# A Conformer layer's depthwise convolution: two channel tiles on TensorE by diagonal matrices become five by quads of taps, and three groups of w_mod go to VectorE

## The chip, the core and the metric

The kernel runs on one core of a Trainium2 chip. The metric is the time of one execution on the device, in microseconds (us). The core's engines are TensorE (PE, matrix products), VectorE (DVE), ScalarE (ACT), GpSimd (POOL) and SyncE (SP, which issues most DMAs). Each has its own queue of instructions and runs it in order; semaphores join them.

## The reference, cut to what matters

Two layers over 256 positions of 2048 channels in float32. Layer 0 mixes positions with a Conformer convolution module, layer 1 with a Mamba-2 mixer; behind each stands a squared-ReLU MLP of 8192 hidden channels. A vector c gives shift, scale and gate of each sub-layer. The change is in layer 0's mixer and in a part of the vectors from c:

```python
mod = (sc @ w_mod[i] + b_mod[i])[:, None, :]            # sc = silu(c)
sh1, sc1, g1, sh2, sc2, g2 = jnp.split(mod, 6, axis=-1)
u = rmsnorm(h, norm_mix_g[i]) * (1 + sc1) + sh1
v = u @ w_pw1 + b_pw1                                   # 2048 -> 4096
a, gt = jnp.split(v, 2, axis=-1)
v = a * jax.nn.sigmoid(gt)
v = causal_dwconv(v, w_dw, b_dw)                        # 31 taps, each channel by itself
v = jax.nn.silu(layernorm(v, ln_g, ln_b))
mix = v @ w_pw2 + b_pw2
h = h + g1 * mix
```

## The kernel before

Channels lie on the 128 partitions and the 256 positions along the free axis, so 2048 channels are sixteen tiles ct of 128x256. The first pointwise product runs in float32 (`native`, L649): eight blocks b of 512 output columns, which are the two halves (value and gate) of two channel tiles. A block has four steps g of four input tiles each, sixteen products, and a 1 MB load `w` from `pw`. Blocks 0 to 2 run while the first shifts and scales arrive; then block 3, and blocks 4 to 7 one after another. `glu` (L567, L569) closes a channel tile: ACT takes the sigmoid of the gate, DVE multiplies and writes to `vpad`, which has 30 zeros ahead of the 256 positions, so that tap k is the slice that begins at k.

`conv(ct)` is the convolution. Of 31 taps ACT makes 24 as scaled copies, four to a 128x1024 buffer (L580), DVE adds these buffers (L596, wide adds), adds the last seven taps one by one (L599), and folds four into one (L603, L605, the adder tree). The last two tiles, 14 and 15, come out of block 7: there PE takes 13 taps as products with diagonal matrices (`diag`, L592), ACT 12 and DVE 6. `close(ct, y)` subtracts a common estimate of the mean, which is tile 0's sum over channels by a product with ones (L614, L616), from each tile (L617), and ACT squares it (L621). `moments` (L631) sums tiles and squares over channels by products with ones, in four column slices of 32, one group of four tiles at a time; the last four tiles are added singly (L737), after the row sums (L726, L730). From these DVE and ACT make mean and deviation (L740 to L748), and `normed` scales, applies the SiLU and splits a group of four tiles into a high and a low part (L757 to L763, L464, L465). The second pointwise product (`pw2`, `outer`, then `block`, L355) multiplies those by split weights (L340, L342).

Beside it runs w_mod: a job is one load of 128x2048 and its product with silu(c). In most groups of four jobs DVE does it in one instruction a job (L271). In the groups listed in PE_GROUPS PE does it with four products of 32 columns and 512 positions (L262), and after the fourth a copy (L268), four transposes (L283) and a sum (L285) bring the row to columns. Jobs are taken from a list, EARLY first: gate g1's groups 0 to 2 and sc2's group 0 beside blocks 3 to 7 (RATE_PW1: 16 jobs in 20 steps), g1's group 3 and sh2's group 0 (BETWEEN: 8 jobs) between the statistics and pw2, and one job a step beside pw2. Before the change all groups of g1 and sh2 of layer 0 are PE's.

All loads of weights go through `stream` (L326) on SP's queue in the order of the program: a load that waits for its buffer, or for its source, holds up those behind it. Buffers are three for `w`, two for `wm`, four for `hid` (w_mod jobs use wm, hid, hid in turn). A scheduler orders each engine's instructions when the program is built, from the order of the code, priorities (`high_priority`) and `issue_after`.

## Time and profile before

| | |
|---|---|
| median of 3 runs | 2610.81 us (2610.38 to 2611.61) |
| the profiled execution | 2609.13 us |
| its span | 2607.2 us, 36320 instructions |
| PE busy | 2541.3 us, 97% |
| DVE, ACT, POOL busy | 1945.7, 1363.9, 132.5 us |
| DMA | 659.10 MB, 253 GB/s in the mean |
| mean granted clock of TensorE | 0.988 |
| PE products of `native` (L649) | 1024 rows, 232.3 us |
| ACT taps (L580) | 360, 148.2 us |

Times are us from the span's start. In a timeline row stand start and length, engine, line, operation, output and inputs, shapes and a count xN; a bracket holds the idle time ahead of it and what ended it. A float32 product shows as two rows of PE, so x32 is sixteen products. A length reaches to the modelled end of a product, and the next one starts before it, so what products cost is read from start to start. In a table of stretches stand length, busy time and count for PE, weight loads, DVE, ACT and POOL, then the granted clock (1.00 is full), the share of time in which the DMA engines were busy, and GB/s.

### The profile page before, as it was taken

What the parts mean: (1) busy time and instruction counts of PE and PEld (TensorE: products, weight loads), DVE (VectorE), ACT (ScalarE), POOL (GpSimd) and SP (SyncE); (2) the same over time, 40 slices, a digit from 0 to 9 for tenths busy, and PEclk for the clock granted to TensorE, in tenths of its full rate; (3) what the DMA queues carried; (4) which work ended last, traced back from release to release, by engine and by line L of the source; (5) the groups of instructions that cost most, each with busy time, mean ns of one, the idle gap of its engine ahead of it and who ended that gap; (6) DMA issues with size and microseconds to landing.
All of it is one profiled execution on the core that took longest, in us unless ns stands there. A gap on an engine that the chain in (4) does not pass through costs nothing.

```text
span 2607.2 us, 36320 instructions
## 1 busy us (share of the span) xinstructions
PE 2541.3 (97%) x14291; PEld 2180.5 (84%) x14291; DVE 1945.7 (75%) x2558; ACT 1363.9 (52%) x2145; POOL 132.5 (5%) x170
## 2 busy tenths in 40 slices
PE   6999999999999999999999999999999999999998
PEld 4877798888888888888888888888998888888886
DVE  6689977677888878887877777888885565565565
ACT  2099754444434434447777666744454344443443
POOL 0000000000000000000000000000000101101000
PEclk8999999999999999999999999999999999999999
DMA  9876797588888888866555455688775555555553
GB/s 406 345 278 252 279 376 285 218 337 320 314 323 328 314 307 334 312 225 220 182 188 184 166 182 182 234 305 317 285 263 189 192 193 190 185 191 194 187 186 144
DMA packets 92878, 659.10 MB, mean 253 GB/s; under 512 B 10497, under 2 KB 10497, under 8 KB 14753
## 3 DMA queue, kind: packets, MB, share of 16 engines
q1 hardware_dynamic: 89138, 644.53, 65.6%
q0 software_dynamic: 3136, 10.59, 1.4%
q8 instruction: 112, 1.84, 0.3%
q10 hardware_dynamic: 432, 1.66, 0.2%
q14 instruction: 60, 0.49, 0.1%
HBM read 654.53 MB, written 2.20 MB: 252 GB/s over the span
## 4 chain that ended last, share of the span: by engine, by line
PE 87%; DVE 6%; DMA 3%; ACT 2%; issue 1%; POOL 0%; ACTq 0%; DVEq 0%; SPq 0%; POOLq 0%
PE mm L355 57%; PE mm L409 8%; PE mm L411 8%; PE mm L410 8%; PE mm L649 3%; ACT taps L580 2%; DMA hid<-wmT 1%; DVE taps L596 1%; DVE wl L342 1%; DVE taps L599 1%; DMA wm<-wmT 1%; DVE hid L271 1%; DVE wm L271 1%; PE ms L262 1%; DMA t<-eac_d 0%
## 5 line engine op out<-in xcount | busy, mean ns | idle before, releaser
L355 PE MATMUL mm<-u,wh 128*128 128x512 f32 (+1 forms) x4544 | 1376.1, 365 | 6.9 <-ACT u L467 3.4
L342 DVE TENSOR_TENSOR wl<-w,wh 128x1024 fp32r<-128x1024 f32 x768 | 940.7, 1228 | 513.5 <-ACT wh L340 510.3
L340 ACT CAST wh<-w 128x1024 fp32r<-128x1024 f32 x768 | 806.8, 1051 | 980.6 <-PE mm L355 602.5
L355 PE MATMUL mm<-u,wl 128*128 128x256 f32 x3840 | 1078.9, 282 | 0.1
L355 PEld LDWEIGHTS mm<-u,wh 128*128 128x128 f32 x4544 | 812.8, 190 | 160.2 <-issue 12.8
L355 PEld LDWEIGHTS mm<-u,wl 128*128 128x128 f32 x3840 | 729.8, 190 | 6.6 <-issue 2.5
L409 PE MATMUL mm<-wh,hid 128*128 128x512 f32 x896 | 350.7, 391 | 0.0
L411 PE MATMUL mm<-wh,hid 128*128 128x512 f32 x896 | 348.8, 389 | 0.0
L410 PE MATMUL mm<-wl,hid 128*128 128x512 f32 x896 | 348.7, 389 | 0.0
L271 DVE SCALAR_TENSOR_TENSOR wm<-wm,scb 128x2048 f32<-128x2048 f32 x128 | 292.3, 2283 | 8.2 <-DMA wm<-wmT 8.2
L649 PE MATMUL mm<-u,w 128*128 128x256 f32 x1024 | 232.3, 388 | 26.7 <-ACT u L560 25.1
L649 PEld LDWEIGHTS mm<-u,w 128*128 128x128 f32 x1024 | 197.6, 195 | 64.9 <-ACT u L560 26.6
L409 PEld LDWEIGHTS mm<-wh,hid 128*128 128x128 f32 x896 | 168.2, 188 | 35.7 <-issue 1.0
L410 PEld LDWEIGHTS mm<-wl,hid 128*128 128x128 f32 x896 | 168.2, 188 | 35.4 <-issue 0.7
L411 PEld LDWEIGHTS mm<-wh,hid 128*128 128x128 f32 x896 | 168.2, 188 | 35.2
L355 PE MATMUL mm<-hid,wh 128*128 128x512 f32 (+1 forms) x576 | 182.5, 373 | 2.4 <-DVE acc L837 2.4
L580 ACT ACTIVATE taps<-u,par 128x256 f32<-128x256 f32 x360 | 148.2, 500 | 3.6 <-DVE taps L596 2.2
L355 PE MATMUL mm<-hid,wl 128*128 128x256 f32 x512 | 143.8, 281 | 0.0
L355 PEld LDWEIGHTS mm<-hid,wh 128*128 128x128 f32 x576 | 104.1, 188 | 23.1 <-DVE acc L837 2.7
L299 POOL TENSOR_TENSOR mod<-mod,par 128x4 f32<-128x4 f32 x46 | 39.8, 864 | 1319.3 <-DVE wm L271 885.1
L355 PEld LDWEIGHTS mm<-hid,wl 128*128 128x128 f32 x512 | 96.9, 189 | 0.4 <-issue 0.2
L596 DVE TENSOR_TENSOR taps<-taps,taps 128x1024 f32<-128x1024 f32 x74 | 90.1, 1218 | 8.7 <-ACT taps L580 7.8
(241 smaller groups left out, 1562.9 us busy)
## 6 DMA issues: line engine op xcount, KB each, us to landing
w<-w SPq DMA_DIRECT2D x256, 1024.0 KB, 4.9
wm<-wmT SPq DMA_DIRECT2D x140, 1024.0 KB, 7.0
w<-win SPq DMA_DIRECT2D x80, 1024.0 KB, 4.9
hid<-wmT SPq DMA_DIRECT2D x52, 1024.0 KB, 10.6
w<-pw SPq DMA_DIRECT2D x48, 1024.0 KB, 5.3
w<-wout SPq DMA_DIRECT2D x32, 1024.0 KB, 6.9
acc<-ac_d POOLq DMA_DIRECT2D x16, 512.0 KB, 7.7
h<-xT SPq DMA_DIRECT2D x4, 512.0 KB, 6.2
```

Source lines behind the costliest of these rows:

```text
L262: self.pe = nc.tensor.matmul(self.row_sums[32 * t:32 * t + 32, :], lhsT=self.scol[:, kt:kt + 1].broadcast_to([P, 32]), rhs=w[:, t * 512:(t ...
L271: self.sum = nc.vector.scalar_tensor_tensor(out=w, in0=w, scalar=1.0, in1=self.scb, op0=ALU.mult, op1=ALU.mult, accum_out=m[:, i:i + 1]).ins
L299: nc.gpsimd.tensor_tensor(out=m, in0=m, in1=b, op=ALU.add)
L340: nc.scalar.copy(out=wh, in_=w[:, s, :])
L342: nc.vector.tensor_tensor(out=wl, in0=w[:, s, :], in1=wh.bitcast(F32), op=ALU.subtract)
L355: self.pe = self.nc.tensor.matmul(out, lhsT=lhsT, rhs=rhs, skip_group_check=True, **kw).ins
L409: mm(banks[q], lhsT=hi, rhs=wh[:, k, :], start=g == 0 and t == 0, stop=False)
L410: mm(banks[q], lhsT=hi, rhs=wl[:, k, :], start=False, stop=False)
L411: mm(banks[q], lhsT=lo, rhs=wh[:, k, :], start=False, stop=g == 3 and t == 3)
L580: st["tap"] = nc.scalar.activation(out=p4[:, q, :], in_=vp[:, k + q:k + q + T], func=AF.Identity, scale=self.col("w_dw", ct * TAPS + k + q ...
L596: nc.vector.tensor_add(wide, wide, products(four("wl"), k))
L649: self.pe = nc.tensor.matmul(o, lhsT=w[:, t, j * P:(j + 1) * P], rhs=u[g][:, t, :], start=g == 0 and t == 0 and j < 2, stop=g == 3 and t == 3,
```

## The change

Five channel tiles, 4, 8, 12, 14 and 15, are convolved on PE alone, all 31 taps and a zero one. For such a tile the 128 rows of a product are 32 channels times four copies of their row, shifted by 0, 8, 16 and 24 taps: `shift` makes the copies with four DMAs from `vpad` to 32 partitions each. The weights (`quad`) hold four taps of each of 32 channels. A tile is eight taps k times four groups c of 32 channels, 32 products of 128 rows, 32 columns and 256 positions (`convolve`); the four groups go to four column slices. The channels of these tiles lie in another order, in which the parameters and the rows of pw2 are laid out on the host. `close` takes PE's result with the bias. The other eleven tiles have 28 taps on ACT and 3 on DVE. PE_GROUPS loses g1's groups 0 to 2, so those twelve jobs are DVE's. Of pw2's first loads one goes ahead of the last shifts, the other two behind four and eight jobs of BETWEEN. The copies use the memory of `xpad`, which layer 1 needs later.

```diff
-ACT_TAPS = 24
-DIAG, PE_TAPS, FEW_TAPS = 2, 13, 12
+ACT_TAPS = 28
+TE_ROWS = (4, 8, 12, 14, 15)
+LONG = T + 7
...
-PE_GROUPS = {(0, G1, g) for g in range(4)} | {(0, SH2, g) for g in range(4)}
+PE_GROUPS = {(0, G1, 3)} | {(0, SH2, g) for g in range(4)}
...
+        self.xpad = self.const("xpad", [P, 5 * (3 + T)])
...
-        W = T + TAPS - 1
+        W = T + TAPS
...
+            nc.gpsimd.memset(v[:, W - 1:], 0.0)
...
+        quad = self.b("acc", [P, 8, P], bufs=5)
+        copies = self.xpad[:, :4 * LONG].rearrange("p (c t) -> p c t", c=4)
+        parts = {}
...
-            with self.tc.high_priority(AHEAD_GLU):
+            with self.tc.high_priority(AHEAD_GLU if ct < NT - 2 else AHEAD_CHAIN):
...
-            few = ct >= NT - DIAG
-            k0, k1 = (PE_TAPS, PE_TAPS + FEW_TAPS) if few else (0, ACT_TAPS)
+            k0, k1 = 0, ACT_TAPS
...
+        def weigh(ct, w):
+            self.stream(w, a["quad"][TE_ROWS.index(ct)])
+        def shift(ct, r):
+            for i in range(4):
+                self.stream(r[32 * i:32 * i + 32], vpad[ct % 12][:, 8 * i:8 * i + LONG])
+        def convolve(ct, w, r):
+            o = parts[ct] = self.bank(self.mm, "mm")[:, :T]
+            with self.tc.issue_after(self.pe):
+                for k in range(8):
+                    for c in range(4):
+                        self.pe = nc.tensor.matmul(o[32 * c:32 * c + 32, :], lhsT=w[:, k, 32 * c:32 * c + 32],
+                                                   rhs=r[:, c, k:k + T], start=k == 0, stop=k == 7,
+                                                   skip_group_check=True).ins
...
-            self.sub = nc.vector.tensor_sub(d, y, st["m0"]).ins
+            if ct in parts:
+                self.sub = nc.vector.scalar_tensor_tensor(out=d, in0=parts[ct], scalar=self.col("b_dw", ct),
+                                                          in1=st["m0"], op0=ALU.add, op1=ALU.subtract).ins
+            else:
+                self.sub = nc.vector.tensor_sub(d, y, st["m0"]).ins
...
+                    if row and g == 2:
+                        weigh(row, quad)
+                        shift(row, copies)
                     load(0, g)
                     self.pump(pump(g))
+                    if row and g == 3:
+                        convolve(row, quad, copies)
+                        if row == 12:
+                            weigh(14, quad)
                     products(0, g, 0, 4)
...
-        native([FIRST], glu, pump=pump, hook=lambda: close(0, y))
...
+        native([FIRST], glu, pump=pump, hook=lambda: close(0, y), row=4)
+        for b, rows in ((4, (1, 2, 3, 4)), (5, (5, 6)), (6, (7, 8, 9)), (7, (10, 11, 13))):
+            for ct in rows:
+                close(ct, None if ct in parts else conv(ct))
             if b >= 6:
                 moments(b - 6)
...
+            native([b], glu, pump=pump, row={5: 8, 7: 12}.get(b))
...
+        there = [self.load_w(a["pw2"][0, 0])]
+        shift(14, copies)
+        quad15 = self.wp.tile([P, 8, P], F32, tag="wh", name=self.nm("taps"), bufs=3)
+        weigh(15, quad15)
+        copies15 = self.b("hid", [P, 4, LONG])
+        shift(15, copies15)
+        close(12, None)
+        convolve(14, quad, copies)
         moments(2)
...
+        rows = self.t("t2", [P, 2 * T], bufs=3)
+        nc.scalar.copy(out=rows, in_=st["sums"])
+        convolve(15, quad15, copies15)
+        close(14, None)
+        close(15, None)
...
-        there = [self.load_w(a["pw2"][b, 0]) for b in range(3)]
...
-            self.pump(BETWEEN)
+            for b in (1, 2):
+                self.pump(BETWEEN // 2)
+                there.append(self.load_w(a["pw2"][b, 0]))
```

How instructions move is seen best in the engines' orders as the program is built. First VectorE at the convolution of tile 0 (`taps_595` before, `taps_609` now; `taps_746` and `taps_790` are tile 1's), before and now:

```order
L596 TENSOR_TENSOR taps_595<-taps_595,taps_618 128x1024
L596 TENSOR_TENSOR taps_595<-taps_595,taps_624 128x1024
L599 SCALAR_TENSOR_TENSOR taps_595<-u_161,par,taps_595 128x256 x7
L596 TENSOR_TENSOR taps_746<-taps_746,taps_751 128x1024
L603 TENSOR_TENSOR taps_595<-taps_595 128x512
L596 TENSOR_TENSOR taps_746<-taps_746,taps_757 128x1024
L605 TENSOR_TENSOR taps_595<-taps_595 128x256
```

```order
L604 TENSOR_TENSOR taps_609<-taps_609,taps_632 128x1024
L282 SCALAR_TENSOR_TENSOR wm_677,mod_679<-wm_677,scb 128x2048
L604 TENSOR_TENSOR taps_609<-taps_609,taps_638 128x1024
L604 TENSOR_TENSOR taps_609<-taps_609,taps_644 128x1024
L607 SCALAR_TENSOR_TENSOR taps_609<-u_162,par,taps_609 128x256 x3
L604 TENSOR_TENSOR taps_790<-taps_790,taps_795 128x1024
L609 TENSOR_TENSOR taps_609<-taps_609 128x512
L604 TENSOR_TENSOR taps_790<-taps_790,taps_801 128x1024
L611 TENSOR_TENSOR taps_609<-taps_609 128x256
```

The first w_mod job (L282, on `wm_677`) now stands ahead of tile 0's last wide adds, of which there is one more, and three single taps remain of seven. Next TensorE from the last step of block 7 to the start of the last statistics (`xpad` are the copies of tile 14, `hid_1758` those of tile 15):

```order
L649 MATMUL mm_1648<-u_164,w_251_1719 128x256 x8
L631 MATMUL ms_1379<-acc_179,ones 32x256 x4
L631 MATMUL ms_1379<-sq_1330,ones 32x256
L631 MATMUL ms_1379<-sq_1377,ones 32x256
L631 MATMUL ms_1379<-sq_1539,ones 32x256
L631 MATMUL ms_1379<-sq_1586,ones 32x256
L592 MATMUL ms_1806<-u_161,hid_1643 128x256 x13
L592 MATMUL mm_1851<-u_162,hid_1645 128x256 x13
L730 MATMUL mm_1894<-t_268_1849,bT_116 128x512
```

```order
L677 MATMUL mm_1614<-u_165,w_245_1684 128x256 x8
L628 MATMUL mm_1766<-xpad,acc_194 32x256 x32
L659 MATMUL ms_1359<-acc_192,ones 32x256 x4
L659 MATMUL ms_1359<-sq_1308,ones 32x256
L659 MATMUL ms_1359<-sq_1357,ones 32x256
L659 MATMUL ms_1359<-sq_1505,ones 32x256
L659 MATMUL ms_1359<-sq_1554,ones 32x256
L628 MATMUL mm_1809<-hid_1758,taps_1756 32x256 x32
L764 MATMUL mm_1848<-t_256_1807,bT_117 128x512
```

The moments of the third group, first before, stand between the two convolutions now, and the row sums (L764, L730 before) behind the second as they did. Last TensorE from the last statistics to pw2's first products (`mm_1997`, `mm_1949`; `ms_` are w_mod's):

```order
L737 MATMUL mm_1894<-nrm_1892,ones 128x256
L262 MATMUL ms_1944<-hid_1941,scol 32x512 x4
L262 MATMUL ms_1944<-wm_1949,scol 32x512 x4
L262 MATMUL ms_1944<-hid_1955,scol 32x512 x4
L262 MATMUL ms_1944<-wm_1961,scol 32x512 x4
L262 MATMUL ms_1972<-hid_1969,scol 32x512 x4
L262 MATMUL ms_1972<-wm_1977,scol 32x512 x4
L355 MATMUL mm_1997<-u_1920,wh_1937 128x256
```

```order
L770 MATMUL mm_1848<-nrm_1846,ones 128x256
L273 MATMUL ms_1892<-hid_1889,scol 32x512 x4
L273 MATMUL ms_1892<-hid_1897,scol 32x512 x4
L273 MATMUL ms_1892<-wm_1903,scol 32x512 x4
L273 MATMUL ms_1892<-hid_1909,scol 32x512 x4
L366 MATMUL mm_1949<-u_1868,wh_1885 128x256
```

Six w_mod jobs stood ahead of pw2's first product, four do now; the other two join the two that stand among the products.

More of the change, by code (lines that the diff above doesn't have):

```diff
@@ L102, in layout @@
     head[:HEADS, 1] = a["mb_a_log"].reshape(-1)
+    order = np.arange(D).reshape(NT, P)
+    for ct in TE_ROWS:
+        order[ct] = order[ct].reshape(32, 4).T.reshape(-1)
+    order = order.reshape(-1)
     par = np.concatenate([
@@ L136, in layout @@
         "wmT": wmt,
[L137 removed]
+        "pw1": _tiles(pw1), "pw2": _tiles(a["cf_w_pw2"][0][order]),
         "wdt": np.ascontiguousarray(wdt.reshape(NT, P, P).transpose(1, 0, 2)),
@@ L987, in mamba @@
         self.time_steps(u)
-        self.xpad = [self.one.tile([P, 3 + T], F32, tag=f"xpad{i}", name=f"xpad{i}") for i in range(5)]
+        self.xpad = [self.xpad[:, i * (3 + T):(i + 1) * (3 + T)] for i in range(5)]
         for v in self.xpad:
```

47 lines of the change are left out of this document (11 added, 36 removed).

## Prediction

> **What bounds the kernel now.** The busy time by stretch comes first, cut where the Conformer's work changes: pointwise blocks 3 to 7 with the convolution, the convolution's tail, the second pointwise product. The columns are TensorE (PE), weight loads, VectorE (DVE), ScalarE (ACT), GpSimd, granted clock, DMA share, GB/s.
>
> ```profile
> 136.00:292.00 156.00, 156.00 (x782) 124.68 (x782) 150.01 (x228) 149.24 (x371) 8.03 (x9) 1.00 0.67 258
> 292.00:311.00 19.00, 17.16 (x88) 13.42 (x86) 16.09 (x29) 13.09 (x30) 0.00 (x0) 1.00 0.82 332
> ...
> 320.00:425.00 105.00, 104.99 (x858) 95.28 (x858) 75.35 (x97) 52.62 (x80) 7.83 (x10) 1.00 0.91 360
> ```
>
> From 136 to 292 three engines are full at once: PE 156.0 us of 156, DVE 150.0, ACT 149.2. Relief for DVE and ACT alone moves nothing there. From 320 to 425 PE is full again, so what the stage wins must survive PE's work behind it. Then the PE timeline of the tail:
>
> ```profile
> 292.23 0.64 PE L631 MATMUL ms<-acc,ones 128*32 128x256 f32 x8
> ...
> 293.23 5.88 PE L592 MATMUL ms<-u,hid 128*128 128x256 f32 x26
> 298.95 5.78 PE L592 MATMUL mm<-u,hid 128*128 128x256 f32 x26
> 304.56 1.02 PE L730 MATMUL mm<-t,bT 128*128 128x512 f32 x2
> 305.42 0.59 PE L737 MATMUL mm<-acc,ones 128*128 128x256 f32 x2
> 305.85 0.59 PE L737 MATMUL mm<-lo,ones 128*128 128x256 f32 x2
> ...
> 310.55 0.61 PE L737 MATMUL mm<-nrm,ones 128*128 128x256 f32 x2
> ...
> 313.69 1.04 PE L262 MATMUL ms<-wm,scol 128*32 128x512 f32 x8
> 314.55 1.04 PE L262 MATMUL ms<-hid,scol 128*32 128x512 f32 x8
> ...
> 320.01 0.39 PE L355 MATMUL mm<-u,wh 128*128 128x256 f32 x1 [0.62 <-DVE u L465]
> ```
>
> Blocks end at 292.23, the two diagonal convolutions at 304.56; the last of eight pairs of statistics (L737) starts at 310.55, and 9.5 us later (320.01) the first normalised tile lets PE run on.
>
> **TensorE until block 7 ends.** The prices are in the timeline's early rows.
>
> ```profile
> 135.90 7.14 PE L649 MATMUL mm<-u,w 128*128 128x256 f32 x32 [1.66 <-DMA w<-pw]
> 142.97 1.06 PE L262 MATMUL mm<-wm,scol 128*32 128x512 f32 x8
> 143.97 7.17 PE L649 MATMUL mm<-u,w 128*128 128x256 f32 x32
> 150.98 0.59 PE L614 MATMUL ms<-taps,ones 128*128 128x256 f32 x2
> ...
> 191.81 0.66 PE L283 MATMUL mm<-ident,t 128*128 128x128 f32 x4
> 192.30 7.07 PE L649 MATMUL mm<-u,w 128*128 128x256 f32 x32
> ```
>
> A step of sixteen products takes 7.0 us (143.97 to 150.98), a w_mod job 1.0 (142.97 to 143.97), the transpose of a job's rows 0.5. Removed before 292: twelve jobs and three transposes, 13.5 us. Added: three convolutions (tiles 4, 8, 12).
>
> A convolution is eight groups of four products with 32 columns each. No row shows one, but w_mod's job is such a group with 512 columns: they follow one another every 0.86 us (313.69 to 314.55), so 0.43 for 256; and the moments (L631), two groups of 256 columns, take 1.00 with the change of kind in it (292.23 to 293.23). A job alone between full products takes 1.00, so going to column slices and back costs 0.14. I take 8 x 0.43 + 0.14 = 3.6 us. Bounds: 3.4 without the 0.14, and 32 x 0.43 = 13.8 if nothing overlapped, from which the 0.86 rows are far. The Trainium skill (TensorEngine Tiling, Key Properties) says that a change of tiling mode drains TensorE, and gives no time. The 0.14 is what these rows leave for it.
>
> New in this stretch is one wait. The first product of statistics (L614) stands behind block 3's second step and needs tile 0's sum. Without the w_mod job PE is there at 135.90 + 14.0 = 149.9. The other engines have more to do first. ACT's timeline, DVE's, DVE's groups in this stage, and the page's group for w_mod:
>
> ```profile
> 134.65 16.56 ACT L580 ACTIVATE taps<-u,par 128x256 f32<-128x256 f32 x41
> ```
> ```profile
> 148.34 0.68 DVE L603 TENSOR_TENSOR taps<-taps 128x512 f32<-128x512 f32 x1
> 148.94 1.22 DVE L596 TENSOR_TENSOR taps<-taps,taps 128x1024 f32<-128x1024 f32 x1
> 150.07 0.42 DVE L605 TENSOR_TENSOR taps<-taps 128x256 f32<-128x256 f32 x1
> ```
> ```profile
> L596 DVE TENSOR_TENSOR taps<-taps,taps 128x1024 f32<-128x1024 f32 x74 | 90.1, 1218 | 8.7 <-ACT taps L580 7.8
> L599 DVE SCALAR_TENSOR_TENSOR taps<-u,par,taps 128x256 f32<-128x256 f32 x110 | 45.1, 477 | 0.4
> ```
> ```profile
> L271 DVE SCALAR_TENSOR_TENSOR wm<-wm,scb 128x2048 f32<-128x2048 f32 x128 | 292.3, 2283 | 8.2 <-DMA wm<-wmT 8.2
> ```
>
> A tap costs ACT 16.56 / 41 = 0.404, a wide add DVE 1.13 (148.94 to 150.07), a half add 0.6, a single tap 45.1 / 110 = 0.41, a w_mod job 2.28. ACT had three taps done by 134.65, so its twentieth is at 141.5. From there DVE's new order is add, w_mod job, two adds, three taps, add, half add, add, quarter add: 1.13 + 2.28 + 2.26 + 1.23 + 1.13 + 0.6 + 1.13 + 0.42 = 10.2, so 151.7. PE waits 1.8 us (0 to 2.5, by how the adds follow ACT).
>
> Block 7's end, E: 135.90 + 20 x 7.0 + 1.8 + 0.6 (L614) + 2.0 (two moments) + 3 x 3.6 = 291.1, where it was 292.23.
>
> **ScalarE and VectorE.** ACT loses 52 of 360 taps, 21 us. DVE goes from 74 to 66 wide adds (-9.0), from 110 to 33 single taps (-31.6) and loses five adder trees (about -5) for twelve w_mod jobs (+27.4). Its list until tile 12 is closed: eleven convolutions at 6 x 1.13 + 3 x 0.41 + 1.3 = 9.3, sixteen jobs at 2.28, 4 us of gates and closes: 143 us from 136.8. With 2 us of early waits and 4 for tile 13, whose taps start only after block 6, it ends near 286. Tile 14's gate is due at E - 2.8 = 288.3: 2 us of cover.
>
> **The loads.** A shift is four DMAs on SP's queue, and each convolution has one of weights: 25 issues in place of 2. The queue's own rows, its longest wait in 100 to 330, and the small landings:
>
> ```profile
> 292.75 0.38 SPq L326 DMA_DIRECT2D hid<-wmT  x1
> ```
> ```profile
> SPq L326 <- PE mm L649: 179.2, 26, 15.2
> ```
> ```profile
> ac_d<-wm POOLq DMA_DIRECT2D x1, 64.0 KB, 3.6
> eac_d<-wm POOLq DMA_DIRECT2D x1, 32.0 KB, 1.8
> ```
>
> At 0.38 us an issue that is 9 us on a queue that waited 179 for PE to free buffers, and 3.6 MB more where DMA was a third idle (0.67). Until block 7 ends it is hidden: the pointwise loads queued behind a shift go out some 20 us (three steps) ahead of use. In the tail it is not. I take 2.5 us from the last issue to landing, between 1.8 and 3.6. Tile 14: gate done at E - 2.3, four issues, landed at E + 1.5. Tile 15: gate done at E + 1.3, landed at E + 5.
>
> **The tail.** PE idles to E + 1.5, convolves tile 14 to E + 5.1, makes the last moments to E + 6.1, convolves tile 15 (landed by then) to E + 9.7; then in order L730 (0.86) and seven pairs (0.43 each). The last pair starts at E + 13.6 = 304.7, where it was 310.55: 5.9 us earlier. The closes of tiles 14 and 15 are hidden by those pairs; what is late next is PE's own list.
>
> **What is given back.** The first normalised tile follows at 304.7 + 9.5 = 314.2. Before it PE did six w_mod jobs, now four, so two (2.0 us) fall into the stretch where PE is full. And the four end at 304.7 + 0.6 + 3.5 = 308.8, so PE stands nearly still for 5.4 us. What that does to the clock shows elsewhere, in the timeline, the stretch and the chain around 430:
>
> ```profile
> 428.58 0.67 PE L482 MATMUL ms<-diag,ones 128*128 128x256 f32 x2 [1.10 <-DVE diag L478]
> ```
> ```profile
> 430.00:440.00 10.00, 9.29 (x54) 8.99 (x55) 8.25 (x12) 3.17 (x6) 0.00 (x0) 0.67 0.54 211
> ```
> ```profile
> 431.94 13.32 PE mm L355 x92
> 445.69 11.51 PE mm L355 x96
> ```
>
> After some 4 us with little more than that 0.67 the clock was 0.67 over the next 10 us, and 92 products took 13.3 us where 96 took 11.5: 2.3 us lost. Between 315.6 and 320, with a w_mod job halfway, it held. The new gap is longer and emptier: I take 2.3, bounds 0 and 3.3.
>
> **Sum:** -5.9 + 2.0 + 2.3 = -1.6 us. The profiled execution took 2609.13 us (span 2607.2); the median of the runs, 2610.81, is 1.7 above. Forecast 2609.2. A measurement of this kernel tells about 0.2%, 5.2 us, from no change, so this is no change. It is passed on whole: PE is full until 425, and the loads keep up (the fourteenth megabyte issued after 294, the first that PE meets in the product's second step, is in by 329 at 2.5 us each, used near 336).
>
> **Rivals.**
> *The tail wins whole.* If the clock holds and tile 0's sum is in time, 2.3 and 1.8 are not lost: -5.7, 2605.1, faster. For it: the gap at 315 kept the clock. Against: the new one has less work in it. 0.18.
> *Column groups overlap by three quarters:* 0.57 a group, five convolutions 5.7 us longer, 2614.9, still no change. The 0.86 rows are against it; that no row has more than five such groups in a line leaves room. 0.10. The Trainium skill (TensorE: Matmul & The Clock Gate, Measured speedup vs the span model) has three column tiles at 2.38 times one, 79%, which would add 4.5 us.
> *Only two of four overlap:* 0.86 a group, 7.0 us a convolution, five times 3.4: +17, 2626, slower. It decides from 5.0 us a convolution on. For it: weights change with every one of the 32 products, four times as many as in the moments. 0.10.
> *VectorE becomes the bound:* a w_mod job stands ahead of adds and gates; if its load is late, ACT's buffers fill and PE waits for gates. Past the 2 us of cover each is one of time, and from 9 late it is slower: 2609 to 2620. For it, 150.0 of 156; against, the shorter list. 0.12, half of it slower.
> *The change doesn't do what it says:* its new order has the jobs off PE and five convolutions on it, which rules this out.
> The forecast has 0.50. Faster 0.18; same 0.50 + 0.10 + 0.06 = 0.66; slower 0.10 + 0.06 = 0.16. Its own range is -5 to +3. To hold 8 in 10 the range takes in a tail with both gains and 1.5 us of earlier landing (2603.5) and most of a late VectorE (2617), and leaves out the 2626.
>
> **What would show it.** Convolutions of 3.6 us, 7 by the third rival; PE idle 1.8 us before its first statistics; block 7 done near 291; the last pair near 304.7; a clock below 1 after 310, held by the first rival; VectorE idle before tile 14's gate, busy up to it by the fourth. I am wrong if PE waits for a load in blocks 3 to 7, or if a shift lands later than 4 us.

## The result, and the profile after

The changed kernel took 2626.49 us (median of six runs, 2623.09 to 2631.66); the kernel before took 2610.60 beside it (2609.96 to 2611.76). The ratio is 1.0062 (95% interval 1.0049 to 1.0076): 16 us slower, where 2609.2 was forecast and no change. The profiled execution took 2630.72 us (span 2628.9), 21.6 more than the one of before, and it is that difference which the traces can explain.

The same three stretches of the kernel after, in the columns of before:

```profile
136.00:292.00 156.00, 144.68 (x760) 121.62 (x761) 139.83 (x168) 134.95 (x337) 5.17 (x6) 0.96 0.70 256
292.00:311.00 19.00, 15.53 (x132) 11.14 (x134) 7.31 (x10) 4.20 (x7) 0.59 (x3) 0.91 0.59 159
320.00:425.00 105.00, 96.58 (x738) 82.71 (x738) 73.07 (x94) 49.21 (x81) 4.91 (x10) 0.95 0.88 343
```

TensorE was full in the first and the third; now it lacks 11.3 and 8.4 us there, and VectorE and ScalarE are less busy than before. So no engine took TensorE's place as the bound: it waits. Where, its timeline tells:

```profile
136.78 14.05 PE L677 MATMUL mm<-u,w 128*128 128x256 f32 x64 [1.88 <-DMA w<-pw]
153.65 1.11 PE L638 MATMUL ms<-taps,ones 128*128 128x256 f32 x2 [2.82 <-DVE taps L611]
154.55 8.39 PE L677 MATMUL mm<-u,w 128*128 128x256 f32 x32
162.88 3.67 PE L628 MATMUL mm<-xpad,acc 128*32 128x256 f32 x64
166.48 48.61 PE L677 MATMUL mm<-u,w 128*128 128x256 f32 x224
222.81 10.17 PE L677 MATMUL mm<-u,w 128*128 128x256 f32 x32 [7.72 <-DMA w<-pw]
232.91 3.67 PE L628 MATMUL mm<-xpad,acc 128*32 128x256 f32 x64
...
297.96 7.17 PE L677 MATMUL mm<-u,w 128*128 128x256 f32 x32
308.60 6.42 PE L628 MATMUL mm<-xpad,acc 128*32 128x256 f32 x64 [3.47 <-DMA xpad<-u]
314.83 0.62 PE L659 MATMUL ms<-acc,ones 128*32 128x256 f32 x8
...
323.26 0.59 PE L770 MATMUL mm<-nrm,ones 128*128 128x256 f32 x2
...
332.76 0.58 PE L366 MATMUL mm<-u,wh 128*128 128x256 f32 x1 [1.69 <-DVE u L476]
...
362.39 0.58 PE L366 MATMUL mm<-u,wl 128*128 128x256 f32 x1 [3.30 <-DVE wl L353]
...
448.60 0.58 PE L502 MATMUL ms<-ones,ssum 128*128 128x1 f32 x4 [0.29 <-DVE ssum L523]
```

A convolution takes 162.88 to 166.48, 3.60 us, as forecast. In block 5 TensorE waits 7.7 us for a pointwise load and then needs 10.1 us for a step of 7.0 (the granted clock was 0.50 from 222 to 228). Block 7 ends (E) at 297.96 + 7.0 = 305.0, not at 291.1. Tile 14's convolution starts 3.6 us later and takes 6.2. The last pair starts at E + 18.3, as far behind E as before (310.55 - 292.23), so the tail won nothing. From the first normalised tile to the end of pw2 (332.76 to 448.60) it is 115.8 us; before it was 105.6 (320.01 to 425.56, where the row of L491 stood that is L502 now).

What held the load of 222.81 is on SP's queue. First SP's timeline, then the group of its waits for VectorE's gates (in all, times, longest), then the gate of tile 8 on ScalarE and on VectorE:

```profile
195.69 0.42 SPq L337 DMA_DIRECT2D acc<-quad  x1
214.72 2.50 SPq L337 DMA_DIRECT2D xpad<-u  x4
217.32 1.03 SPq L337 DMA_DIRECT2D w<-pw  x2
...
298.47 0.43 SPq L337 DMA_DIRECT2D w<-pw  x1
302.74 2.50 SPq L337 DMA_DIRECT2D xpad<-u  x4
306.19 2.52 SPq L337 DMA_DIRECT2D hid<-u  x4
308.76 1.08 SPq L337 DMA_DIRECT2D hid<-wmT  x2
```
```profile
SPq L337 <- DVE u L585: 31.4, 5, 18.6
```
```profile
213.13 0.45 ACT L583 ACTIVATE a<-mm,par 128x256 f32<-128x256 f32 x1
```
```profile
214.19 0.47 DVE L585 SCALAR_TENSOR_TENSOR u<-mm,par,a 128x256 f32<-128x256 f32 x1
```

SP stands at tile 8's shift from 196 to 214.7, 18.6 us, until VectorE has made the gate; only then the load of block 5's third step goes out, at 217.3, and TensorE wanted it at 215.1 (222.81 - 7.72). Block 4 had ended at about 201.5 (five steps behind 166.48): the gate (214.2) came 12.7 us behind that. The gate stands behind taps in ScalarE's list. Block 3's first gate, before and after:

```profile
164.46 0.46 ACT L567 ACTIVATE a<-mm,par 128x256 f32<-128x256 f32 x1
```
```profile
185.01 0.47 ACT L583 ACTIVATE a<-mm,par 128x256 f32<-128x256 f32 x1
```

In the tail the same queue stands at the shifts of tiles 14 and 15, from 298.9 to 308.7, with all of pw2's and w_mod's loads behind them. There tile 14's gate is in time (SP has it at 302.7, E - 2.3); 5.0 of these 9.8 us are the eight issues themselves, 0.63 us each (2.50 and 2.52 for four), where the forecast took 0.38.

Ahead of that, from about 281.5 to 298.1, SP stands at tile 14's weights, whose buffer tile 12's convolution still reads (16.6 us). The stretch from 290 to 300:

```profile
290.00:300.00 10.00, 10.00 (x94) 7.35 (x93) 8.27 (x12) 0.83 (x2) 0.59 (x3) 1.00 0.06 15
```

The DMA engines were 0.06 busy (15 GB/s); before, they were 0.66 busy in these ten microseconds. That this makes TensorE wait at 362 is not shown. What TensorE lacks there is VectorE's half of a split (L353), which stands behind three w_mod jobs (L282) in VectorE's list:

```profile
354.06 2.28 DVE L282 SCALAR_TENSOR_TENSOR wm<-wm,scb 128x2048 f32<-128x2048 f32 x1
...
356.69 2.29 DVE L282 SCALAR_TENSOR_TENSOR hid<-hid,scb 128x2048 f32<-128x2048 f32 x1
...
358.90 2.28 DVE L282 SCALAR_TENSOR_TENSOR hid<-hid,scb 128x2048 f32<-128x2048 f32 x1
...
361.12 2.35 DVE L353 TENSOR_TENSOR wl<-w,wh 128x1024 fp32r<-128x1024 f32 x2
```

ScalarE's half of the same split begins at 355.63, so the load was there by then, and TensorE wanted the other half at 359.1. In the kernel before, the jobs come one by one between the splits (327.90, 331.25, 334.59), and TensorE waits for none.

**Theory.** The shifts put results of compute into an in-order queue of loads. A gate that is late, which no load waited for before, now holds back every load behind it. **Rival.** VectorE's list is the bound and SP only passes its lateness on.

### The profile page after: what moved, and what is told of

Its sections match the earlier page's. It is cut to its first block, busy times and chain, and to the rows that moved or that the text cites. A ratio compares the mean times of both kernels' runs of the same rounds, so it can differ in the third digit from the quotient of the medians.

```text
span 2628.9 us, 36563 instructions
## 1 busy us (share of the span) xinstructions
PE 2547.3 (97%) x14451; PEld 2185.7 (83%) x14451; DVE 1929.9 (73%) x2482; ACT 1340.9 (51%) x2090; POOL 127.9 (5%) x182
## 4 chain that ended last, share of the span: by engine, by line
PE 89%; DMA 4%; DVE 3%; ACT 3%; issue 1%; SPq 0%; POOL 0%; ACTq 0%; DVEq 0%
PE mm L366 58%; PE mm L422 8%; PE mm L420 8%; PE mm L421 8%; PE mm L677 4%; ACT taps L595 2%; DMA hid<-wmT 2%; DMA wm<-wmT 1%; PE mm L628 1%; PE ms L273 1%; DVE hid L282 1%; PE ms L1247 1%; DVE wl L353 1%; DMA acc<-ac_d 0%; DVE wm L282 0%
## 5 line engine op out<-in xcount | busy, mean ns | idle before, releaser
L353 DVE TENSOR_TENSOR wl<-w,wh 128x1024 fp32r<-128x1024 f32 x768 | 941.0, 1228 | 520.2 <-ACT wh L351 516.8
L282 DVE SCALAR_TENSOR_TENSOR wm<-wm,scb 128x2048 f32<-128x2048 f32 x132 | 301.5, 2284 | 7.9 <-DMA wm<-wmT 7.7
L595 ACT ACTIVATE taps<-u,par 128x256 f32<-128x256 f32 x308 | 126.4, 499 | 7.2 <-DVE u L585 5.8
L366 PEld LDWEIGHTS mm<-hid,wh 128*128 128x128 f32 x576 | 104.9, 190 | 24.5 <-DVE acc L872 3.2
L282 DVE SCALAR_TENSOR_TENSOR hid<-hid,scb 128x2048 f32<-128x2048 f32 x40 | 91.1, 2284 | 27.3 <-DMA hid<-wmT 27.2
## 6 DMA issues: line engine op xcount, KB each, us to landing
xpad<-u SPq DMA_DIRECT2D x16, 131.5 KB, 3.6
```

The source lines that it names most:

```text
L282: self.sum = nc.vector.scalar_tensor_tensor(out=w, in0=w, scalar=1.0, in1=self.scb, op0=ALU.mult, op1=ALU.mult, accum_out=m[:, i:i + 1]).ins
L353: nc.vector.tensor_tensor(out=wl, in0=w[:, s, :], in1=wh.bitcast(F32), op=ALU.subtract)
L366: self.pe = self.nc.tensor.matmul(out, lhsT=lhsT, rhs=rhs, skip_group_check=True, **kw).ins
L595: st["tap"] = nc.scalar.activation(out=p4[:, q, :], in_=vp[:, k + q:k + q + T], func=AF.Identity, scale=self.col("w_dw", ct * TAPS + k + q ...
```

## The experiments

Each is timed against the kernel before in the same group; e1 to e4, e5 to e8, e9 to e11 and e12 to e14 shared its runs (2610.1, 2609.9, 2609.6, 2609.4 us). Where an edit is to the kernel with the loads ahead, it is to e1.

**e1: the loads ahead of the shift.**

```diff
+                    load(0, g)
+                    self.pump(pump(g))
                     if row and g == 2:
                         weigh(row, quad)
                         shift(row, copies)
-                    load(0, g)
-                    self.pump(pump(g))
```

> The changed kernel with one order swapped: in the third step of blocks 3, 5 and 7 the step's pointwise load (and its w_mod load) goes on SP's queue ahead of the convolution's weights and its four shift DMAs, not behind them. Theory: the 7.7 us in which TensorE waited for a load at 215 to 223 came from the load standing behind tile 8's shift, which waited 18.6 us for VectorE's gate; with it go the 7.7 and the 3.1 us at half clock behind it, so block 7 ends near 294 in place of 305.0, and the time is 2626.5 - 10.8 = 2615.7 (2613 to 2618). Rival: VectorE is the bound and SP only passes its lateness on; TensorE then waits as long for tile 8's copies or for a gate, block 7 still ends at 303 or later, and the time stays over 2623.

2620.67 us, 1.0043 (1.0030 to 1.0057). TensorE's timeline:

```profile
217.31 3.68 PE L628 MATMUL mm<-xpad,acc 128*32 128x256 f32 x64
...
278.77 3.67 PE L628 MATMUL mm<-xpad,acc 128*32 128x256 f32 x64
...
297.45 5.34 PE L628 MATMUL mm<-xpad,acc 128*32 128x256 f32 x64 [7.92 <-DMA xpad<-u]
```

The wait in block 5 is gone, the waits at the first statistics too (the gates now stand further ahead in ScalarE's and VectorE's lists: tile 6's at 176.4 in place of 187.1), and E is 278.77 + 3.6 + 7.0 = 289.4: 15.6 us earlier, and earlier than the 291.1 of the forecast. The theory holds for that wait: tile 8's gate (204.7) still comes 8 us behind block 4's end (161.86 + 35.0), and no load waits for it. But the edit also changed the lists, so the 15.6 us are not the queue's alone. And 4.4 us come back at once: tile 14's copies are there at E + 8.0, since its gate (291.0 on VectorE) now comes later than E. ScalarE says why:

```profile
287.66 0.42 ACT L649 ACTIVATE nrm<-acc 128x256 f32<-128x256 f32 x1 [5.52 <-DVE acc L645]
290.20 0.42 ACT L649 ACTIVATE lo<-acc 128x256 f32<-128x256 f32 x1 [2.13 <-DVE acc L642]
290.53 0.82 ACT L583 ACTIVATE a<-mm,par 128x256 f32<-128x256 f32 x2
```

The gate (L583) stands behind the squares of tiles 13 and 12, which wait for VectorE. And pw2 still takes 116.5 us.

**e2: pw2's loads back ahead of the w_mod jobs.**

```diff
+        there += [self.load_w(a["pw2"][b, 0]) for b in (1, 2)]
...
-            for b in (1, 2):
-                self.pump(BETWEEN // 2)
-                there.append(self.load_w(a["pw2"][b, 0]))
+            self.pump(BETWEEN)
```

> The changed kernel with the second and third load of the second pointwise product's weights ahead of the eight w_mod jobs between statistics and product, where they stood before the change. Theory: the 3.6 us wait for the split of the second load (behind 362 in the trace) and some 1.8 us at a lower clock behind it go: 2626.5 - 5.4 = 2621 (2619 to 2623). Rival: VectorE is late for the split by its own list, and the time stays at 2626.

2629.58 us, 1.0078 (1.0064 to 1.0092): nothing won. VectorE's half of the split is waited for less (1.7 us), and two jobs' loads (1.1 and 1.4) and ScalarE's half (1.2) are waited for instead:

```profile
324.44 1.94 PE L273 MATMUL ms<-wm,scol 128*32 128x512 f32 x8 [1.44 <-DMA wm<-wmT]
...
358.88 0.58 PE L366 MATMUL mm<-u,wl 128*128 128x256 f32 x1 [1.73 <-DVE wl L353]
```

The theory had put the wait down to the load alone; the split still stands behind w_mod jobs in VectorE's list (the last of them at 355.38, the split at 357.60), which is nearer to the rival. With pw2's loads ahead, the jobs' loads are late.

**e3: three jobs in TensorE's wait ahead of tile 14.**

```diff
+        with self.tc.issue_after(self.pe):
+            self.pump(3)
         there = [self.load_w(a["pw2"][0, 0])]
         shift(14, copies)
```

> The changed kernel with three more w_mod jobs taken right behind block 7: their loads go ahead of tile 14's shift, their products on TensorE into its 3.5 us wait for tile 14's copies. Theory: the lower clock of tile 14's convolution (6.2 us for 3.6) comes from that wait; with 3.0 us of products in it the convolution takes 3.6, and three fewer jobs stand in the stretch behind: 2626.5 - 2.6 - 3.0 = 2621 (2619 to 2624). Rival: the jobs' loads come too late or hold the copies up, the convolution starts as much later, and the time stays at 2624 or more.

2632.28 us, 1.0087 (1.0072 to 1.0103): the rival. TensorE runs the jobs, waits for their loads, and then longer for the copies:

```profile
312.72 5.35 PE L628 MATMUL mm<-xpad,acc 128*32 128x256 f32 x64 [4.91 <-DMA xpad<-u]
```

SP issued the last of tile 14's four copies at 302.0: they took 10.7 us from there, where in the changed kernel they took 3.4 (305.2 to 308.6). Ahead of them four loads of 1 MB had been issued, from 295.2 to 297.2.

**e4: e1, e2 and e3 together.** The three diffs above.

> The three edits of the other kernels of this group together. Theory: they mend separate stretches, so the gains add: 2626.5 - 10.8 - 5.4 - 5.6 = 2604.7 (2602 to 2609), below the 2610.6 of the kernel before, which would show that five tiles on TensorE and twelve jobs on VectorE pay once the loads are in time. Rival: VectorE is the bound, and what one edit wins the next wait takes: 2613 or more.

2619.82 us, 1.0038 (1.0023 to 1.0052): the rival. Only e1's gain is left of the three; the copies took 6.6 us (294.1 to 300.7).

**e5: the shifts on GpSimd's queue.**

```diff
-                self.stream(r[32 * i:32 * i + 32], vpad[ct % 12][:, 8 * i:8 * i + LONG])
+                nc.gpsimd.dma_start(out=r[32 * i:32 * i + 32], in_=vpad[ct % 12][:, 8 * i:8 * i + LONG])
```

> The changed kernel with all twenty shift DMAs on GpSimd's queue in place of SP's; loads and weights stay on SP. Theory: a shift on SP's queue holds back every load behind it until VectorE has made the gate. Off that queue the wait of 7.7 us in block 5 and its 3.1 us at half clock go, and the second product's loads go out near 295 in place of 309, so that its wait of 3.6 us and the lower clock behind it go too: 2626.5 - 10.8 - 5.4 = 2610.3 (2606 to 2615). Rival: VectorE's and ScalarE's lists are what is late; the queue only shows it. Then TensorE waits for gates and copies instead, as the kernel with the loads ahead did (7.9 us for tile 14's copies), and the time stays at 2618 or more.

2626.72 us, 1.0070 (1.0057 to 1.0082): in time the rival, in the trace something else. The wait in block 5 is gone (E at 286.02 + 10.6 = 296.6), and pw2's and w_mod's loads go out from 290 on, as the theory had it. Then tile 14's copies, issued by 298.5, land at 310.5:

```profile
310.47 5.18 PE L628 MATMUL mm<-xpad,acc 128*32 128x256 f32 x64 [13.67 <-DMA xpad<-u]
```

The stretch in between:

```profile
300.00:310.00 10.00, 0.00 (x0) 0.00 (x0) 0.00 (x0) 0.00 (x0) 0.62 (x2) 0.50 1.03 229
```

No engine does anything; the DMA engines are full, and move 229 GB/s where loads alone move 420 (320 to 330 in the changed kernel). By queue (packets, MB, share of 16 engines) the loads are the first row, the copies the second:

```profile
q1 hardware_dynamic: 221, 1.67, 74.7%
q0 software_dynamic: 211, 0.62, 27.9%
```

Both are slow: 1.67 MB in 74.7% of ten microseconds are 224 GB/s, 0.62 MB in 27.9% are 222. The copies are of rows of 263 floats, 1052 bytes. Copies alone are not that slow: in e1, from 291.8 to 294.0, nothing but tile 14's copies was in flight, and they moved 0.27 MB in 38.9% of 2.2 us, 315 GB/s. So most of the fall comes with the mixing, to loads and copies alike; why, no run shows. The Trainium skill (DMA: Bandwidth & Descriptors, Why small descriptors are slow) says that copies within SBUF are spared the penalty of small pieces. The 315 are a quarter below the 420 of loads all the same, and no run changed the rows' size. So freeing the queue alone only moves the loss: the loads that then go ahead delay the copies. And though pw2's loads now go out 48 us ahead of its first normalised tile (338.37), TensorE still waits 2.0 us for splits there, again behind w_mod jobs.

**e6: two blocks' gates ahead of taps.** In the fragment, `open` is VectorE's part of a gate.

```diff
-                close(ct, None if ct in parts else conv(ct))
+                with self.tc.issue_after(st["gate"]) if ct in (3, 6) else nullcontext():
+                    with self.tc.issue_after(st["open"]) if ct in (3, 6) else nullcontext():
+                        y = None if ct in parts else conv(ct)
+                close(ct, y)
```

> The changed kernel with SP's order as it is, but tile 3's convolution on ScalarE and VectorE ordered behind the gates of block 3 (tiles 6, 7), and tile 6's behind those of block 4 (tiles 8, 9). In the changed kernel these gates stand behind taps and adds that are not needed yet: block 4 ends near 201, its first gate is done at 214.7. Theory: with tile 8's gate done by 205 its shift and the load behind it go out in time, and the 7.7 us and the 3.1 behind it go, as with the loads ahead: 2620 (2616 to 2623). Rival: the gates are late because VectorE has too much to do, not by their place; then they stay late or the pinned lists wait elsewhere, and the time is 2625 or more.

2625.31 us, 1.0064 (1.0052 to 1.0076), which its expectation gave to the rival; the wait for the load falls from 7.7 to 3.3 us, as the gate of tile 8 moves from 214.2 to 209.8 only. The queue's order is the changed kernel's here, so that is the link from gate to load, one for one: 4.4 us off the one, 4.4 off the other. The first gate of block 3 now has 84 taps ahead of it, not 118, and is late all the same:

```profile
177.01 0.42 ACT L650 ACTIVATE sq<-acc 128x256 f32<-128x256 f32 x1 [6.33 <-DVE acc L646]
179.62 0.42 ACT L650 ACTIVATE lo<-acc 128x256 f32<-128x256 f32 x1 [2.19 <-DVE acc L643]
179.94 0.46 ACT L583 ACTIVATE a<-mm,par 128x256 f32<-128x256 f32 x1
```

The taps are gone from ahead of it, two squares are left, and those wait for closes that stand behind w_mod jobs on VectorE. The edit was too weak to show the kernel with its gates in time.

**e7: the convolution alone.**

```diff
-PE_GROUPS = {(0, G1, 3)} | {(0, SH2, g) for g in range(4)}
+PE_GROUPS = {(0, G1, g) for g in range(4)} | {(0, SH2, g) for g in range(4)}
```

> The changed kernel with all groups of g1 and sh2 on TensorE as before the change, so that only the convolution differs from the kernel before: 13.5 us of w_mod work come back to TensorE before block 7 ends, 27.4 leave VectorE. Theory: VectorE is then never late, tile 8's gate comes when block 4 ends, and no load waits behind a shift: 2626.5 + 13.5 - 10.8 = 2629 (2624 to 2634). Rival: the shift holds the loads up whatever VectorE does, and the wait of 7.7 us stays: 2638 or more.

2639.23 us, 1.0111 (1.0096 to 1.0126): the rival. VectorE is 114.5 us busy of 156, and TensorE still waits in block 5:

```profile
226.49 3.78 PE L677 MATMUL mm<-u,w 128*128 128x256 f32 x8 [6.02 <-DMA w<-pw]
```

Tile 8's gate on ScalarE comes behind 41 taps without a pause:

```profile
200.50 11.36 ACT L595 ACTIVATE taps<-u,par 128x256 f32<-128x256 f32 x28
...
212.16 5.28 ACT L595 ACTIVATE taps<-u,par 128x256 f32<-128x256 f32 x13
217.35 0.45 ACT L583 ACTIVATE a<-mm,par 128x256 f32<-128x256 f32 x1
```

VectorE has the gate at 217.8, 13.6 us behind block 4's end (204.2), against 12.7 in the changed kernel (214.2 and 201.5). So the gate is late by its place in ScalarE's list, and no relief of VectorE mends that.

**e8: the jobs alone.** The same line of the kernel before, edited the other way.

```diff
-PE_GROUPS = {(0, G1, g) for g in range(4)} | {(0, SH2, g) for g in range(4)}
+PE_GROUPS = {(0, G1, 3)} | {(0, SH2, g) for g in range(4)}
```

> The kernel before with only the other half of the change: three groups of g1 on VectorE, the convolution as it was. TensorE loses 13.5 us of work before block 7 ends; VectorE, 150.0 us busy of 156 there, gets 27.4 more. Theory: VectorE becomes the bound of the stretch, which then takes some 177 us, and the gates are late: 2610.6 + 21 = 2632 (2622 to 2640). Rival: VectorE's busy time holds slack that the new order uses, and the time is within 5 of 2610.6.

2627.41 us, 1.0070 (1.0058 to 1.0082): here VectorE is the bound (153.4 of 156 busy), and TensorE waits for its closes up to the last statistics, whose last pair starts 19.1 us later than before (329.61 for 310.55):

```profile
318.38 1.22 PE L737 MATMUL mm<-acc,ones 128*128 128x256 f32 x2 [7.22 <-DVE acc L617]
```

Each half of the change alone costs 17 to 29 us; together they cost 16. By the busy times above each relieves the engine that the other loads.

**e9: four jobs in place of eight ahead of pw2 (on e1).**

```diff
-BETWEEN = 8
+BETWEEN = 4
```

> The kernel with the loads ahead of the shifts (2620.7), and four w_mod jobs in place of eight between the statistics and the second pointwise product; the other four, and with them all later jobs, come four places later. Theory: what that kernel still loses, some 11 us between its first normalised tile and the product's end, is late loads: the tail's shifts hold SP up to 297 while the DMA engines are 0.42 busy, and then fifteen megabytes come at once. With four megabytes less ahead of the product's second and third load its waits for the split (3.3 and 0.3 us) and the lower clock behind them go: 2620.7 - 5.4 = 2615.3 (2611 to 2617). Rival: it is not the amount but the place, the loads wait for their buffers; then the waits stay and the time is 2619 or more.

2615.16 us, 1.0020 (1.0011 to 1.0029): 5.5 won, in size the theory. From the first normalised tile to pw2's end it is 104.9 us (320.95 to 425.81) for 116.5: the waits for splits are gone, and four jobs fewer stand there, which come back later beside a full TensorE. Whether the theory's cause is the right one is open, because the edit changes two things: four megabytes less stand ahead of pw2, and on VectorE the three jobs that stood in a row ahead of the split (in e1 from 341.27 to 348.33) now come one by one between splits (346.74, 353.68, 359.44).

**e10: unread products in TensorE's empty stretches (on e1).**

```diff
+        def warm(n):
+            o = self.bank(self.ms, "ms")[:, :T]
+            with self.tc.issue_after(self.pe):
+                for _ in range(n):
+                    self.pe = nc.tensor.matmul(o, lhsT=self.ones, rhs=u[3][:, 0, :], start=True, stop=True).ins
...
+        warm(16)
         convolve(14, quad, copies)
...
+        warm(7)
         with self.tc.issue_after(self.pe):
```

> The kernel with the loads ahead of the shifts (2620.7), with products whose result nobody reads put into TensorE's two empty stretches: sixteen (7.0 us) ahead of tile 14's convolution, seven (3.1 us) behind the last statistics. Nothing else changes. Theory: the clock falls in the empty stretches (tile 14's convolution 5.2 us for 3.6, the first normalised tiles' products at half speed up to 324); with TensorE busy it holds: 2620.7 - 1.6 - 2.5 = 2616.6 (2614 to 2618). Rival: the clock falls for another reason, or comes back as late whatever TensorE did before; 2620 or more.

2615.45 us, 1.0023 (1.0014 to 1.0032), in size the theory. The first stretch works: tile 14's convolution takes 3.5 us for 5.2, 1.7 won:

```profile
296.49 3.67 PE L628 MATMUL mm<-xpad,acc 128*32 128x256 f32 x64 [0.96 <-DMA xpad<-u]
```

The second hardly does: the products behind the first normalised tile (318.04) still run at half speed up to 322 (to 325 in e1), and from that tile to pw2's end it is 116.2 us for 116.5. So some 2.0 of the 5.2 us are the edit's. At pw2's end the kernel is 2.8 us ahead of e1 (434.26 for 437.04), but 0.9 of these it had at E already, ahead of the edit; the rest came later in the program. In both places the two kernels are the same, so it is luck in part that the time fits the theory.

**e11: two jobs fewer on VectorE before E (on e1).**

```diff
-RATE_PW1 = spread(16, 20)
-BETWEEN = 8
+RATE_PW1 = spread(14, 20)
+BETWEEN = 10
```

> The kernel with the loads ahead of the shifts (2620.7), with fourteen w_mod jobs beside blocks 3 to 7 in place of sixteen; the last two of VectorE's go behind the statistics, where VectorE has idle time. Theory: with the loads in time VectorE is the next bound: tile 14's gate is done at 291.5, due at 286.6 when TensorE makes its half of the bank, because tile 13's adds and the last jobs stand ahead of it. With 4.6 us less on VectorE the gate comes near 287.5, TensorE's wait for tile 14's copies falls from 7.9 to some 4, and the time to 2616.7 (2614 to 2619). Rival: ScalarE's order of taps sets the gate, not VectorE's load; the wait stays at 7 or more and the time at 2620 or more.

2620.20 us, 1.0043 (1.0031 to 1.0055): by the time the rival, but the wait of 6.4 us for 7.9 lies between the two. With 4.6 us less work on VectorE the gate moves by 2.5, from 291.0 to 288.5. With two jobs more ahead of pw2 it is then 122.1 us from the first normalised tile to its end (318.44 to 440.51) for 116.5.

**e12: what stands ahead of tile 14's gate goes behind it (on e1).** `open` holds the two instructions of a gate; the jobs come in seventeen steps.

```diff
-                close(ct, None if ct in parts else conv(ct))
+                y = None if ct in parts else conv(ct)
+                if ct < 13:
+                    close(ct, y)
...
-        close(12, None)
+        sig, mul = st["open", 14]
+        with self.tc.issue_after(sig), self.tc.issue_after(mul):
+            close(12, None)
+            close(13, y)
...
-RATE_PW1 = spread(16, 20)
+RATE_PW1 = spread(16, 17) + [0] * 3
```

> The kernel with the loads ahead of the shifts (2620.7), with what stands ahead of tile 14's gate taken from there: the closes of tiles 12 and 13 are ordered behind it on ScalarE and VectorE, and the sixteen w_mod jobs come in the first seventeen of the twenty steps, so that none is left in block 7's last three. Theory: VectorE's load does not make that gate late, its place does; the gate goes from 291.5 to about 287, tile 14's copies are there near 293 in place of 297.4, and the time is 2620.7 - 4.4 = 2616.3 (2614 to 2619). Rival: ScalarE and VectorE are simply full up to there; the gate moves by less than 2 and the time stays at 2619 or more.

2613.39 us, 1.0014 (1.0004 to 1.0024): the theory, and 2.9 us better than it said. The gate comes at 286.24, and TensorE waits as in the changed kernel, now with E at 289.0:

```profile
292.66 5.35 PE L629 MATMUL mm<-xpad,acc 128*32 128x256 f32 x64 [3.52 <-DMA xpad<-u]
```

VectorE does as much work up to E as in e1 (145.1 us from 136 on, for 144.8). So it was the place: 4.8 us for the gate, where less work brought 2.5 (e11).

**e13: e1, e9, e10 (with eight and seven products) and e12 together.**

> Together: loads ahead of the shifts, the closes behind tile 14's gate and no job in block 7's last steps, four w_mod jobs in place of eight between statistics and second product, and unread products in TensorE's two empty stretches (eight and seven). Theory: the gains of 4.4, 5.5 and 5.2 add to those of the swapped loads: 2620.7 - 15 = 2605.6 (2603 to 2609), so the change does pay, by 4 to 5 us, once its waits are gone. Rival: each mend shows the next wait and the time stays at 2611 or more, no faster than the kernel before.

2607.52 us, 0.9992 (0.9983 to 1.0000). TensorE:

```profile
293.28 3.67 PE L629 MATMUL mm<-xpad,acc 128*32 128x256 f32 x64
...
418.73 0.58 PE L502 MATMUL ms<-ones,ssum 128*128 128x1 f32 x4
```

The clock holds in both stretches (1.00 from 288 to 326). pw2 ends 6.8 us earlier than before the change (425.56), but four jobs have moved behind it, which alone end it 3.1 us earlier in the old kernel (422.48 in e14); 1.9 us are left by the medians, within what a measurement tells. So the time lies in the theory's range and the 16 us are made up, by edits two of which (fewer jobs, unread products) go beyond the change; that the change pays is not shown even then.

**e14: the edit of e9 on the kernel before.**

> The kernel before the change with one edit: four w_mod jobs in place of eight between the statistics and the second product. Theory: there the loads are in time and TensorE waits for none of them, so the edit moves jobs and wins nothing: 2610 (2608 to 2612), and what it wins on the changed kernel is a cost of the change. Rival: fewer megabytes there help the old kernel as well, by 3 or more: 2607 or less, and the mended kernel would have to be held against that.

2610.58 us, 1.0006 (0.9997 to 1.0015): nothing, as the theory said. What e9 mends on the changed kernel belongs to the change.

## Why the prediction was wrong

**What failed** is a sentence on the loads: "Until block 7 ends it is hidden: the pointwise loads queued behind a shift go out some 20 us (three steps) ahead of use." The 20 us (17.5 in the trace of before: issued at 143.07, used at 160.60) were those of a queue that waits for PE's buffers; a shift waits for a gate, and the gate was taken to come when its block ends. In the trace of before gates did: block 3's first stands at 165.24, 2.5 us ahead of that block's end. The change moved them: ScalarE has 73 taps ahead of it in the trace of before and 118 in that of after (0.40 us each, 18 us). ScalarE's order was not weighed; the text ahead of the prediction gives VectorE's and TensorE's only. So the step that failed is the load wait in block 5, put at 0: it was 7.7 us, with 3.1 more at the lower clock behind it. That the queue carries a late gate to the load is shown by e1 (the load ahead of the shift, no wait) and e6 (4.4 us off the gate, 4.4 off the wait); that VectorE's load is not what makes tile 8's gate late, by e7. Why the scheduler set the gates so late was not tried.

Point by point, on the profiled execution:

| step | forecast | trace of after |
|---|---|---|
| a convolution at full clock | 3.6 | 3.60 |
| start of block 3 | 135.9 | 136.8 |
| wait at the first statistics, and the clock behind it | 1.8 | 2.8 + 1.3 |
| wait for a load in block 5, and the clock behind it | 0 | 7.7 + 3.1 |
| E | 291.1 | 305.0 |
| tile 14's copies there | E + 1.5 | E + 3.6 |
| tile 14's convolution | 3.6 | 6.2 |
| last pair | E + 13.6 | E + 18.3 |
| from there to the first normalised tile | 9.5 | 9.5 |
| first normalised tile to pw2's end, against before | +4.3 | +10.3 |

The 13.9 us of E are 0.9 + 1.0 + 1.3 + 7.7 + 3.1 (14.0). The 4.7 us of the tail are two mis-sized terms: a shift lands 3.4 us behind its last issue (305.24 to 308.60) where 2.5 was taken, and four issues take 2.50 us where some 1.3 were taken, 1.2 more; the convolution behind the gap runs at half clock (0.50 from 308 to 314), 2.6 us, where the loss was put only behind the statistics. The last row holds the 2.0 and 2.3 that were forecast for the two jobs and the clock, and some 6 us that were not: 3.6 of waits for splits (3.3 and 0.3), some 1.5 of half clock behind the longer one (0.50 from 362 to 364), and a rest without a place. The forecast put nothing for these splits. Its sentence "the loads keep up" fell in so far as SP stood at tile 14's weights and at the shifts until 308.7, where loads were taken to go out behind 294; but in the trace TensorE waits for no load there, only for VectorE behind its three w_mod jobs. Neither e2 nor e5 got rid of the wait by earlier loads. Sum: 13.9 + 4.7 + 6.0 over the forecast's -1.6 makes +23.0, which is what pw2's end shows (448.60 for 425.56); 1.4 came back later.

**The rivals.** Groups of columns that overlap by half would have given 2626, near the measured time, and are wrong all the same: 3.60 us a convolution at full clock rules them out. The Trainium skill's 2.38 for three column tiles (TensorE: Matmul & The Clock Gate, Measured speedup vs the span model), from which the forecast worked out 4.5 us for five convolutions, is not what this trace shows either. VectorE as the bound was half right: it was not in the changed kernel (139.8 of 156 busy, and e7), but is in e8. That the tail wins whole fell with E and the copies. The chance given to slower, 0.16, hung on causes that did not occur, and the case that did had none; the text named it only among what would make it wrong, a load that TensorE waits for in blocks 3 to 7.

**What stays open.** e6 did not bring the gates where they were due, so nothing shows the changed kernel with its own queue order and gates in time. Some 3 of the 5.2 us that e10 won have no place in the stretches that it edits, and the clock held behind 1.7 us of idle time in e13 (up to 315.49) but not in e10 (up to 318.04). Whether late loads or the place of the w_mod jobs makes pw2 10 us longer is not decided.

## What to carry to other kernels

Before a transfer of a computed tile goes on a queue of prefetched loads, find where its producer stands in each engine's list after the change, not when it was done before: the loads behind it are as late as it is. Moving the transfer to another queue is no cure by itself, since the loads then compete with it; what has to be counted is the bytes that the next stretch needs and the free time of the DMA engines just before. And an engine's busy share does not show that its results come in time: here a change of place moved a gate by 4.8 us (e12), while 4.6 us less work moved it by 2.5 (e11), and 25 us less left another as late as it was (e7).

## What the runs showed of the hardware that was not expected

Copies from SBUF to SBUF, four of 131.5 KB in rows of 1052 bytes, were there 3.4 us behind their last issue when only the 0.5 MB of tile 15's weights went out right behind them (305.24 to 308.60; the same in e1 and e12), and 6.6, 10.7 and 12.0 us when four (e4, e3) or six (e5) loads of 1 MB had been issued in the 12 us before. Alone they moved 311 to 315 GB/s of full DMA engines (0.30 MB in 53.6% of 303.5 to 305.3 in the changed kernel; 0.27 MB in e1), against 420 of loads. Mixed with a load, both together moved about half: 213 GB/s from 305 to 309 in the changed kernel, 229 in e5. An issue of such a copy held SP for 0.60 to 0.63 us, one of a load for 0.33 to 0.43.

Thirty-two products of 32 columns in four column slices, with other weights for each, took 3.60 us: eight groups of 0.43 and 0.14 by the forecast's prices. So four of them cost no more than one product of 128 columns (0.44, a step of 7.0 over sixteen).

A gap of 3.5 us on TensorE cost the convolution behind it 1.7 us in e12 (5.14 to the next row, 292.66 to 297.80, for 3.45 in e13) and 2.8 in the changed kernel (6.23). The granted clock shows the difference: in half-microsecond stretches it was at half for 3.41 us in e12, beginning 1 us after the convolution had started, and for 6.82 in the changed kernel. Every stretch at half clock from 140 to 380 in the changed kernel, e1, e5 and e9 to e12 lasted 3.41, 6.82, 10.24 or 13.65 us: one, two, three or four times 3.41, whatever the gap. In the kernel before and in e13 there was none. The Trainium skill (TensorE: Matmul & The Clock Gate, What's actually happening) says that about the first 3.4 us of work behind an idle stretch run at half clock. By an estimate from that figure 1.7 us are lost, which e12 agrees with and the changed kernel, with 5.6 us of work at half clock, exceeds.
